# Lower bounds of a gated recurrence made as columns, and its first projection placed ahead of the compression of keys

## The chip, the cores and the metric

One core of a Trainium2 chip runs the whole program. The metric is the device time of one execution in microseconds (us). The core has five engines: PE (TensorE, the matrix products), DVE (VectorE), ACT (ScalarE), POOL (GpSimd) and SP (SyncE, which here only issues DMAs). Each takes its own instructions in order; semaphores make one wait for another.

## The reference

The program is three transformer-like blocks with a mixture of experts and a retrieval layer between them. The change lies in the mixer of the second block alone: 256 tokens of width 1024, an attention over compressed, selected and windowed keys, and beside it a gated recurrence.

```
lb_all = cumsum(softmax(hgrn_lb_logits, axis=0), axis=0)     # logits [2, 512]; row 0 is used
# compression of keys: blocks of positions + pos_emb, then gelu(flat @ w1) @ w2
# recurrence, 4 heads of 128, chunks of 32 tokens:
f = lb + (1 - lb) * sigmoid(hf);  k = 1 - f;  q = silu(hq)
b = cumsum(log f) in the chunk
o = tril(q e^b (k e^-b)^T) v + q e^b S
S = e^b_end * S + (k e^(b_end-b))^T v
o = rmsnorm(o) * norm_g * silu(hg)
y = g_a * (o_nsa @ w_branch[0]) + g_b * (o @ w_branch[1]);  out = y @ w_out
```

hq, hf, hi, hg and the two gates are columns of one projection of the normed input. With a softmax over two rows, lb is one row of 512 numbers, the same for every token.

## The kernel before

Activations lie with tokens on partitions (two halves of 128 tokens, index `a`). Every weight matrix comes by SP's queue in pieces of 1 MB into a ring of six buffers. `dense` takes one piece of 128x1024 at a time: ACT casts it to a rounded half `wh` (L151), DVE subtracts to get the rest `wl` (L152), and PE multiplies both with the split activations (L169: `pd<-wh,b`, `pd<-wl,b`, 128x512 each), 12 matmuls for a piece, 48 for a projection of 512 columns.

`block2` holds two generators. `attention()` begins with the key compression: transposes of keys (L1192, L1208), copies out of them into a padded tile (L1195 and L1213 on DVE), the addition of the position embedding (L1218, DVE), and 2 x 16 products with the first compression matrix (L1221; the DVE tile of L1218 is the weight side, so L1221 waits for it). Then come four head pairs of softmax and products. `recurrence()` first makes lb and 1 - lb in the scaled form `lb[0]`, `om` from two rows that DMAs spread over all partitions (L1333 to L1344), then four projections in the order f, q, v, g (`c` = 1, 0, 2, 3), and then for each half `a` the chunks: products with the state `S` (L1412, which waits for `S`), the update of `S` (L1417 on PE; L1419, L1420 on DVE), and at the end of the half a norm: Square on ACT (L1424), sum and scaling on DVE (L1426, L1427), a power on POOL (L1428), three products on DVE (L1430 to L1432), transposes on PE (L1435) and copies out of PSUM (L1438 ACT, L1439 DVE) into `OHT`. The four gate projections and the branch projections (L1462 on; `ONT`, the attention's output, and `OHT`, the recurrence's) follow.

Beside them runs `fill`: the next adaptive modulation, summed by ACT (L291), DVE (L292) and additions `acc + t` of 128x1024 (L294), of which six in eight are on POOL, and reduced by PE (L265, L270).

In what order the instructions of an engine stand is set by a scheduler that takes dependences and the order of the code; the code of the second block is written as `attention()` to its end, then `recurrence()` to its end, then gates. In the order of instructions a tile's name carries a number that differs between the two kernels.

Of the kernel before, what the change touches and what calls it, by code (L numbers as in the profile page):

```python
# [12 lines left out]
AF = mybir.ActivationFunctionType  # L13
ALU = mybir.AluOpType
AX = mybir.AxisListType
PSUM = bass.MemoryType.PSUM
P = 128
# [11 lines left out]
def bcast_rows(ap1d, n=P):  # L29

    return ap1d.unsqueeze(0).broadcast_to([n, ap1d.shape[-1]])
# [23 lines left out]
def step(gen, n):  # L55
    for _ in range(n):
        next(gen, None)


def body(tc, A, out, stages=("b1", "moe", "b2", "peer", "b3"), dbg=None):  # L60
# [31 lines left out]
    with Pool("cst") as cst, Pool("ring", bufs=RING) as ring, Pool("psum", nb={"ps": 4, "pd": 3, "pa": 1}, space=PSUM) as psp:  # L92
# [398 lines left out]
        if "b2" in stages:  # L491
            block2(K)
# [635 lines left out]
def block2(K):  # L1128
    nc, mm, pst, psd, A, x, ident, cst, Pool = K.nc, K.mm, K.pst, K.psd, K.A, K.x, K.ident, K.cst, K.Pool
    col, load, load8, mod = K.col, K.load, K.load8, K.mods[2]  # L1130
    nb = {"b8": 5, "b4": 5, "b2": 4, "h2": 7, "wh": 2, "wl": 2}
    with Pool("b2", nb=nb) as wp:
# [196 lines left out]
        lb = [wp("lb", [P, 512], bufs=2) for _ in range(2)]  # L1329

        def recurrence():
            for r in range(2):
                nc.sync.dma_start(lb[r], bcast_rows(A["hgrn_lb"][r]))  # L1333
            om = wp("h2", [P, 512])
            nc.vector.tensor_tensor(om, lb[0], lb[1], ALU.max)
            for r in range(2):
                nc.vector.tensor_tensor(lb[r], lb[r], om, ALU.subtract)
                nc.scalar.activation(lb[r], lb[r], AF.Exp)
            nc.vector.tensor_tensor(om, lb[0], lb[1], ALU.add)
            nc.vector.reciprocal(om, om)  # L1340
            nc.vector.tensor_tensor(lb[0], lb[0], om, ALU.mult)

            nc.vector.tensor_scalar(om, lb[0], -0.5, 0.5, ALU.mult, ALU.add)
            nc.vector.tensor_scalar(lb[0], lb[0], 0.5, 0.5, ALU.mult, ALU.add)  # L1344
            for c in (1, 0, 2, 3):
                w = load8(A["w_in_2"][2 + c])
                for a, ps in enumerate(K.dense(wp, [hT], w)):
# [7 lines left out]
                    else:  # L1355
                        d = (HQ if c == 0 else HG)[:, a, :]
                        t = wp("h2", [P, 512])
# [18 lines left out]
            for a in range(2):  # L1376
# [18 lines left out]
                for src, dst in ((qd, qdT), (ki, kiT)):  # L1395
                    pt = pst()
# [12 lines left out]
                for c in range(4):  # L1409
                    r = slice(32 * c, 32 * c + 32)  # L1410
# [22 lines left out]
                pt = pst()  # L1433
# [11 lines left out]
        def gates(h, j):  # L1445
# [3 lines left out]
            for a, ps in enumerate(K.dense(wp, [hT], w)):  # L1449
                nc.scalar.activation(G[j][:, a, h * 512 : (h + 1) * 512], ps, AF.Tanh, scale=0.5)  # L1450

        for _ in attention():
            pass
        for _ in recurrence():
            pass
        for h in range(2):
            for j in range(2):
# [4 lines left out]
        for h in range(2):  # L1462
            w = load8(A["w_branch"][h])
            for j, o in enumerate((ONT, OHT)):
                for a, ps in enumerate(K.dense(wp, [o], w, k0=4 * j, kt=4)):
                    m = M[:, a, h * 512 : (h + 1) * 512]
                    t = wp("b2", [P, 512]) if j else m
# [471 lines left out]
def _chunk(w, n=512):  # L1939

    k, m = w.shape
    return np.ascontiguousarray(w.reshape(k // P, P, m // n, n).transpose(2, 1, 0, 3))


def _cols(v):
    return np.ascontiguousarray(v.reshape(-1, P).T)
# [68 lines left out]
def layout(I):  # L2015
    f = lambda n: np.asarray(I[n])
    A = {}
    A["x"] = f("x")[0]
    A["ctx"] = f("ctx")[0]
    cols = []  # L2020
    for n in _COL_NAMES:
        v = f(n)
        if n in ("conv_w_3", "ffn_conv_w_3"):
            v = v[0].reshape(3, -1, P).transpose(2, 0, 1).reshape(P, -1)
        else:
            v = _cols(v.reshape(-1))
        cols.append(v)
    A["p_cols"] = np.ascontiguousarray(np.concatenate(cols, axis=1))
    A["w_ada"] = _chunk(f("w_ada")[0][:, 0:2048].reshape(D, 2, 4, 256).transpose(0, 2, 1, 3).reshape(D, 2048))
    A["w_ada_g"] = _chunk(f("w_ada")[0][:, 2048:], 2048)  # L2030
    A["b_ada"] = f("b_ada")[0]
    A["b_in"] = f("b_in")[0]
    A["w_in"] = _chunk(f("w_in")[0])
    A["attn_sink"] = f("attn_sink")[0]
    A["w_pool"] = np.ascontiguousarray(f("w_pool")[0].reshape(4, 2, P, T).transpose(2, 0, 1, 3))
    for n in ("w_attn_br", "w_pool_br", "w_out"):
        A[n] = _chunk(f(n)[0])
    A["w_router"] = np.ascontiguousarray(f("w_router")[0].reshape(8, P, 32).transpose(1, 0, 2))
    A["b_router"] = f("b_router")[0]
    A["b_gu"] = f("b_gu")[0]  # L2040
    A["b_down"] = f("b_down")[0]
    A["w_gu"] = np.ascontiguousarray(f("w_gu")[0].reshape(32, 8, P, 4, 512).transpose(0, 3, 2, 1, 4))
    A["w_down"] = np.ascontiguousarray(f("w_down")[0].reshape(32, 8, P, 2, 512).transpose(0, 3, 2, 1, 4))
    A["final_g"] = f("final_g")
    A["w_ada_2"] = _chunk(f("w_ada_2")[0], 2048)
    A["b_ada_2"] = f("b_ada_2")[0]
    w = f("w_in_2")[0]
    o = 512 + 768 + 24
    A["w_in_2"] = _chunk(np.concatenate([w[:, 0:1024], w[:, o : o + 4096]], axis=1))
    A["w_in_2b"] = np.ascontiguousarray(w[:, 1024:o].reshape(8, P, 280).transpose(1, 0, 2))  # L2050
    pe = np.stack([f("cmp_pos_k_2")[0], f("cmp_pos_v_2")[0]])
    A["cmp_pos"] = np.ascontiguousarray(pe.reshape(2, 16, P).transpose(2, 0, 1))
    A["w_c1"] = np.ascontiguousarray(np.stack([f("w_ck1_2")[0], f("w_cv1_2")[0]]).reshape(2, 16, P, P).transpose(0, 2, 1, 3))
    A["w_c2"] = np.ascontiguousarray(np.stack([f("w_ck2_2")[0], f("w_ck2_2")[0], f("w_cv2_2")[0]], axis=1))
    A["hgrn_lb"] = f("hgrn_lb_logits_2")
    A["hgrn_norm"] = f("hgrn_out_norm_2")[0]
    A["w_branch"] = _chunk(f("w_branch_2")[0].reshape(1024, D))
    A["w_out_2"] = _chunk(f("w_out_2")[0])
    A["w_peer_q"] = _chunk(f("w_peer_q_2")[0])
    A["peer_keys"] = np.ascontiguousarray(f("peer_sub_keys_2")[0].transpose(3, 1, 0, 2).reshape(P, 16, P))  # L2060
    u = f("peer_u_2")[0].reshape(P, 32, 4, 8, P)
    A["peer_u"] = np.ascontiguousarray(u.transpose(1, 4, 2, 3, 0).reshape(32, P, 4, D))
    A["peer_v"] = np.ascontiguousarray(f("peer_v_2")[0].reshape(P, 32, 4, D).transpose(1, 0, 2, 3))
    A["g_final_2"] = f("g_final_2")
    A["w_ada_3"] = _chunk(f("w_ada_3")[0], 2048)
    A["b_ada_3"] = f("b_ada_3")[0]
    A["w_in_3"] = _chunk(f("w_in_3")[0])
    A["w_out_3"] = _chunk(f("w_out_3")[0])
    w = f("w_up_3")[0].reshape(8, P, 2, 11, 2 * P)
    A["w_up_3"] = np.ascontiguousarray(w.transpose(3, 1, 0, 2, 4).reshape(11, P, 8, 512))  # L2070
    A["w_down_3"] = np.ascontiguousarray(f("w_down_3")[0].reshape(11, 2, P, D).transpose(0, 2, 1, 3))
    A["g_final_3"] = f("g_final_3")
    A.update(constants())
    return A
# [19 lines left out]
```

## Time and profile before

| | |
|---|---|
| median of three runs | 2760.5 us (2754.87 to 2763.53) |
| profiled execution | 2761.05 us, of which the span is 2759.3 us |
| busy over the span | PE 93%, DVE 56%, ACT 37%, POOL 8% |
| mean granted TensorE clock | 0.974 |
| DMA queue, share of 16 engines | 74.9% |

The second block's mixer lies between about 1280 and 1557 us of the span. A group of a timeline is several instructions of one kind that follow each other; the brackets at its end give how long the engine stood idle ahead of it and what it waited for. A granted clock of 1.00 is TensorE's level of 2.4 GHz, 0.50 its level of 1.2 GHz.

### The profile page before, as it was taken

The page shows a single profiled execution, that of the slowest core. Times are in us where ns is not written, and L with a number is a line of the kernel's source. Part 1 is how long each engine was busy: PE and PEld are TensorE (multiplying, and loading weights), DVE is VectorE, ACT ScalarE, POOL GpSimd, SP SyncE. Part 2 cuts the span into 40 slices and gives each one's busy share as a digit, 9 for nine tenths or more (in the row PEclk, how much of TensorE's full clock was granted, in tenths as well). Part 3 has the DMA queues.
Part 4 walks back from the last instruction along what each step waited for, and adds up shares of the span by engine and source line. Part 5 has one row for each costly group of instructions (what it writes and reads, how often), then busy time and mean ns, then how long its engine had stood idle before and what let it go on. Part 6 is the DMA issues. An engine that isn't in the chain of part 4 may idle for free. (4 is left out here: it accounts for less than half of the span.)

```text
span 2759.3 us, 36658 instructions
## 1 busy us (share of the span) xinstructions
PE 2572.4 (93%) x14235; PEld 1776.8 (64%) x14235; DVE 1532.0 (56%) x2573; ACT 1023.2 (37%) x1604; POOL 207.4 (8%) x125
## 2 busy tenths in 40 slices
PE   7999997999799969998999998999999999999998
PEld 4767741333133313333766897999888888888897
DVE  4997621122112202114787799697777675567777
ACT  3665300010001000002564433875555444455554
POOL 1221000000000000001112022100101000010000
PEclk9999999999999989999999999999999999999999
DMA  7669699999999999998565443678887775554452
GB/s 288 233 227 331 263 388 424 424 422 373 423 424 423 406 424 424 423 424 323 170 211 200 152 159 132 214 228 321 280 294 282 252 288 198 197 181 138 168 184 77
DMA packets 154016, 786.02 MB, mean 285 GB/s; under 512 B 14960, under 2 KB 49648, under 8 KB 70000
## 3 DMA queue, kind: packets, MB, share of 16 engines
q1 hardware_dynamic: 153840, 783.66, 74.9%
q8 instruction: 113, 1.85, 0.3%
q14 instruction: 63, 0.52, 0.0%
HBM read 765.78 MB, written 17.83 MB: 284 GB/s over the span
## 5 line engine op out<-in xcount | busy, mean ns | idle before, releaser
L152 DVE TENSOR_TENSOR wl<-w,wh 128x1024 fp32r<-128x1024 f32 x361 | 456.6, 1270 | 166.0 <-ACT wh L151 156.6
L151 ACT CAST wh<-w 128x1024 fp32r<-128x1024 f32 x379 | 393.8, 1044 | 344.1 <-PE pd L169 108.2
L169 PE MATMUL pd<-wh,b 128*128 128x512 f32 (+1 forms) x960 | 266.3, 395 | 2.2 <-POOL b L419 0.8
L936 PE MATMUL pd<-w,xd 128*64 128x512 f32 (+2 forms) x864 | 242.6, 601 | 4.6 <-DMA w<-in_w_gu 4.6
L169 PEld LDWEIGHTS pd<-wh,b 128*128 128x128 f32 x960 | 176.3, 189 | 48.0 <-issue 8.6
L1707 PE MATMUL pd<-wh,b 128*128 128x512 f32 x630 | 194.5, 390 | 0.2 <-ACT b L1691 0.2
L902 DVE TENSOR_SCALAR b<-pd 128x512 f32<-128x512 f32 x28 | 19.4, 692 | 254.5 <-PE pd L937 254.5
L169 PE MATMUL pd<-wl,b 128*128 128x512 f32 (+1 forms) x480 | 152.2, 396 | 5.8 <-DVE wl L152 5.7
L936 PEld LDWEIGHTS pd<-w,xd 128*64 128x64 f32 (+2 forms) x864 | 71.7, 132 | 113.9 <-issue 101.8
L936 PE MATMUL pd<-wB,xd 128*64 128x512 f32 (+2 forms) x392 | 137.0, 611 | 4.0 <-DMA wB<-in_w_gu 4.0
L955 DVE TENSOR_TENSOR b<-pd,g 128x512 f32<-128x512 f32 x28 | 19.3, 691 | 212.2 <-PE pd L937 212.2
L901 ACT ACTIVATE b<-b 128x512 f32<-128x512 f32 x28 | 17.7, 632 | 309.7 <-DVE b L900 309.7
L1707 PEld LDWEIGHTS pd<-wh,b 128*128 128x128 f32 x630 | 115.9, 188 | 22.9 <-ACT b L1691 0.4
L936 PE MATMUL pd<-w,at 128*64 128x512 f32 (+2 forms) x384 | 115.0, 646 | 14.1 <-DMA w<-in_w_down 13.4
L936 PE MATMUL pd<-wA,xd 128*64 128x512 f32 (+2 forms) x272 | 113.4, 647 | 4.9 <-DMA wA<-in_w_gu 4.9
L893 ACT ACTIVATE xd<-ps,mod,gs 128x128 f32<-128x128 f32 x56 | 25.3, 460 | 240.0 <-PE ps L889 160.2
L900 DVE TENSOR_SCALAR b<-pd 128x512 f32<-128x512 f32 x28 | 19.3, 690 | 165.1 <-PE pd L937 165.1
L169 PEld LDWEIGHTS pd<-wl,b 128*128 128x128 f32 x480 | 88.8, 189 | 28.3 <-DVE wl L152 8.3
L1707 PE MATMUL pd<-wl,b 128*128 128x512 f32 x315 | 105.5, 389 | 0.0
L1575 DVE TENSOR_TENSOR b<-iota,slt 128x512 f32<-128x512 f32 x128 | 87.1, 736 | 22.7 <-PE pd L1583 22.7
L1669 PE MATMUL ps<-b,wh 128*128 128x256 f32 x384 | 96.4, 292 | 2.8 <-ACT wh L151 2.8
L152 DVE TENSOR_TENSOR xT<-w,xT 128x1024 fp32r<-128x1024 f32 x53 | 66.3, 1251 | 55.9 <-ACT xT L151 55.9
(621 smaller groups left out, 5673.4 us busy)
## 6 DMA issues: line engine op xcount, KB each, us to landing
w<-in_w_gu SPq DMA_DIRECT2D x108, 1024.0 KB, 19.2
w<-in_peer_u SPq DMA_DIRECT2D x64, 1024.0 KB, 5.2
w<-in_peer_v SPq DMA_DIRECT2D x64, 1024.0 KB, 5.2
w<-in_w_down SPq DMA_DIRECT2D x59, 1024.0 KB, 19.6
w<-in_w_in SPq DMA_DIRECT2D x50, 1024.0 KB, 5.8
wB<-in_w_gu SPq DMA_DIRECT2D x49, 1024.0 KB, 19.6
w<-in_w_ada SPq DMA_DIRECT2D x48, 1024.0 KB, 6.0
wA<-in_w_gu SPq DMA_DIRECT2D x34, 1024.0 KB, 19.5
```

Of the source, the lines that this page charges most:

```text
L151: nc.scalar.copy(h, raw)
L152: (eng or nc.vector).tensor_tensor(l, raw, h.bitcast(F32), ALU.subtract)
L169: ins = mm(o, h[:, kk - k0 + k, a * P : (a + 1) * P], w[:, k * n : (k + 1) * n], start=(kk == k0 and m == 0 and k == 0), stop=(kk == k0 + ...
L893: nc.scalar.activation(d, s, AF.Identity, bias=sh[:, q : q + 1], scale=gs[:, q : q + 1])
L900: nc.vector.tensor_scalar(g, psg, 7.0, None, ALU.min)
L901: nc.scalar.activation(s, g, AF.Tanh, scale=0.851)
L902: nc.vector.tensor_scalar(l, psl, 7.0, -7.0, ALU.min, ALU.max)
L936: mm(ps[r], xt[:, k, r], ws[i][k // 4][:, k % 4, :], start=(k == 0), stop=False, skip_group_check=True)
L955: nc.vector.tensor_tensor(y, ps, g2[:, c * 512 : (c + 1) * 512], ALU.mult)
L1575: nc.vector.tensor_tensor(o, iota.unsqueeze(1).broadcast_to([P, 4, P]), SLT[:, v, t0 : t0 + 4].unsqueeze(2).broadcast_to([P, 4, P]), ALU.i ...
L1669: mm(o, wh[:, c], hh[:, k, :], start=(k == 0), stop=False)
L1707: ins = mm(acc[2 * a + c], p[:, i, a * P : (a + 1) * P], q[:, c * 512 : (c + 1) * 512], start=(first and i == 0 and n == 0), stop=(last an ...
```

## The change

The logits come as columns: one DMA brings a tile of 128 x 2 x 4, feature on partition. The softmax and the two scaled forms are worked out on 4 or 8 columns. Eight PE transposes of a column spread over 128 columns give the two rows on all partitions, and two ACT copies take them from PSUM to `lb[0]` and `om`. The generator of the recurrence is made before the attention's and taken one step, so that the lower bounds and the projection for f come ahead of the key compression in the code.

```
-            for r in range(2):
-                nc.sync.dma_start(lb[r], bcast_rows(A["hgrn_lb"][r]))
+            lc = wp("lc", [P, 2, 4])
+            nc.sync.dma_start(lc, A["hgrn_lb"])
+            mo = wp("lo", [P, 2, 4])
+            nc.vector.tensor_tensor(mo[:, 0, :], lc[:, 0, :], lc[:, 1, :], ALU.max)
+            nc.vector.tensor_tensor(lc, lc, mo[:, 0:1, :].broadcast_to([P, 2, 4]), ALU.subtract)
+            nc.scalar.activation(lc, lc, AF.Exp)
+            nc.vector.tensor_tensor(mo[:, 0, :], lc[:, 0, :], lc[:, 1, :], ALU.add)
+            nc.vector.reciprocal(mo[:, 0, :], mo[:, 0, :])
+            nc.vector.tensor_tensor(lc[:, 0, :], lc[:, 0, :], mo[:, 0, :], ALU.mult)
+            nc.vector.tensor_scalar(mo[:, 0, :], lc[:, 0, :], 0.5, 0.5, ALU.mult, ALU.add)
+            nc.vector.tensor_scalar(mo[:, 1, :], lc[:, 0, :], -0.5, 0.5, ALU.mult, ALU.add)
             om = wp("h2", [P, 512])
-            nc.vector.tensor_tensor(om, lb[0], lb[1], ALU.max)
...
-            nc.vector.tensor_scalar(om, lb[0], -0.5, 0.5, ALU.mult, ALU.add)
-            nc.vector.tensor_scalar(lb[0], lb[0], 0.5, 0.5, ALU.mult, ALU.add)
+            for r, t in enumerate((lb[0], om)):
+                pt = pst()
+                for k in range(4):
+                    nc.tensor.transpose(pt[:, k * P : (k + 1) * P], mo[:, r, k : k + 1].broadcast_to([P, P]), ident)
+                nc.scalar.copy(t, pt)
...
+        linear = recurrence()
+        step(linear, 1)
         for _ in attention():
             pass
-        for _ in recurrence():
+        for _ in linear:
             pass
...
-    A["hgrn_lb"] = f("hgrn_lb_logits_2")
+    A["hgrn_lb"] = np.ascontiguousarray(f("hgrn_lb_logits_2").reshape(2, 4, P).transpose(2, 0, 1))
```

In the changed file the lines of the recurrence have numbers 6 higher from its projections on (L1412 is L1418, L1435 is L1441), those behind `attention()`'s call 8 higher (L1468 is L1476). Outside the second block's mixer the order of instructions is the same on every engine.

On PE, at the key compression, this stands before. `b_1519` and `b_1520` are the two split halves of the input, `pd_7989` and `pd_7990` the projection that follows.

```order
L1192 MATMUL ps_7447<-ident_64,b_1532_7175 128x128 x4
L1192 MATMUL ps_7457<-ident_64,b_1532_7175 128x128 x4
L1208 MATMUL ps_7474<-ident_64,b_1533_7176 128x128 x4
L169 MATMUL pd_7989<-wh_7991,b_1519_7124 128x512 x2
L169 MATMUL pd_7989<-wh_7991,b_1520_7125 128x512 x2
L169 MATMUL pd_7990<-wh_7991,b_1519_7124 128x512 x2
L169 MATMUL pd_7990<-wh_7991,b_1520_7125 128x512 x2
L1221 MATMUL ps_7470<-w_7471,b_1601_7479 32x128 x16
```

The same place in the changed kernel, from the last transposes of keys to the first product of the compression; ahead of it stand the eight transposes of L1349 and the 48 matmuls for f.

```order
L1208 MATMUL ps_7574<-ident_64,b_1533_7176 128x128 x4
L169 MATMUL pd_8076<-wh_8078,b_1519_7124 128x512 x2
...
L169 MATMUL pd_8077<-wl_8095,b_1519_7124 128x512 x2
L169 MATMUL pd_8076<-wh_8110,b_1519_7124 128x512
L1221 MATMUL ps_7570<-w_7571,b_1618_7579 32x128 x16
```

Between L1208 and L1221 there were 8 matmuls, and there are 25 now.

On POOL, between the key compression and the end of the recurrence, the additions of `fill` and the recurrence's memsets (L1400) and powers (L1428) stood like this before.

```order
L294 TENSOR_TENSOR b_1529_7170<-b_1529_7170,w_8595 128x1024
L294 TENSOR_TENSOR b_1824_8617<-b_1824_8617,w_8693 128x1024
L294 TENSOR_TENSOR b_1824_8617<-b_1824_8617,w_8698 128x1024
L1400 MEMSET h_1766_8325 128x512
L294 TENSOR_TENSOR b_1844_8720<-b_1844_8720,w_8795 128x1024
L294 TENSOR_TENSOR b_1844_8720<-b_1844_8720,w_8800 128x1024
L1428 TENSOR_TENSOR ss_8400<-ss_8400,mhalf_70 128x4
L294 TENSOR_TENSOR b_1863_8822<-b_1863_8822,w_8897 128x1024
L1400 MEMSET h_1791_8436 128x512
L294 TENSOR_TENSOR b_1863_8822<-b_1863_8822,w_8902 128x1024
L1428 TENSOR_TENSOR ss_8503<-ss_8503,mhalf_70 128x4
```

In the changed kernel they stand like this.

```order
L294 TENSOR_TENSOR b_1828_8628<-b_1828_8628,w_8709 128x1024
L294 TENSOR_TENSOR b_1848_8731<-b_1848_8731,w_8806 128x1024
L294 TENSOR_TENSOR b_1848_8731<-b_1848_8731,w_8811 128x1024
L294 TENSOR_TENSOR b_1867_8833<-b_1867_8833,w_8908 128x1024
L294 TENSOR_TENSOR b_1867_8833<-b_1867_8833,w_8913 128x1024
L1406 MEMSET h_1770_8336 128x512
L1434 TENSOR_TENSOR ss_8411<-ss_8411,mhalf_70 128x4
L1406 MEMSET h_1795_8447 128x512
L1434 TENSOR_TENSOR ss_8514<-ss_8514,mhalf_70 128x4
```

Four of the eight additions have moved from the recurrence to ahead of it, into the head pairs of the attention.

On PE, at the end of the recurrence's second half, this stood before; `oT_7434` and `oT_7435` are `ONT`, `b_1519` belongs to a gate projection.

```order
L1412 MATMUL ps_8456<-S_8494,h_1789_8434 32x128 x4
L169 MATMUL pd_8830<-wl_8880,b_1519_7124 128x512
L306 MATMUL pd_8913<-ident_64,mod_9_83 128x128 x4
L306 MATMUL pd_8919<-ident_64,mod_9_83 128x128 x4
L169 MATMUL pd_8930<-wh_8932,oT_7434 128x512 x2
...
L169 MATMUL pd_8930<-wh_8948,oT_7435 128x512
L1435 MATMUL ps_8510<-ident_64,h_1802_8501 128x128 x4
```

In the changed kernel `oT_7436` and `oT_7437` are `OHT`; `pd_8987` and `pd_8988` are its branch projection for the two halves.

```order
L1418 MATMUL ps_8467<-S_8481,h_1793_8445 32x128 x4
L1423 MATMUL ps_8500<-hp_7440,h_1792_8438 128x128 x4
L169 MATMUL pd_8987<-wl_9006,oT_7436 128x512
L1418 MATMUL ps_8467<-S_8493,h_1793_8445 32x128 x4
L1418 MATMUL ps_8467<-S_8505,h_1793_8445 32x128 x4
L1441 MATMUL ps_8521<-ident_64,h_1806_8512 128x128 x4
L373 MATMUL ps_9109<-ident_64,b_1886_8936 128x128
L373 MATMUL ps_9116<-ident_64,b_1886_8936 128x128
L169 MATMUL pd_8988<-wh_8989,oT_7436 128x512 x2
```

The gate projections and the whole branch projection of `ONT` stand ahead of this place now, and between the last product with `S` and the transposes of the norm's result nothing is left.

On DVE, the same place in the changed kernel: L1425 and L1426 make `S`, L1432 to L1438 are the norm, L1476 and L1478 take a branch projection out of PSUM.

```order
L1425 TENSOR_TENSOR S_8493<-S_8481,dec_8434 128x512
L1426 TENSOR_TENSOR S_8493<-S_8493,ps_8488 128x512
L1476 SCALAR_TENSOR_TENSOR b_1903_9021<-b_1829_8631,pd_8987 128x512
L1425 TENSOR_TENSOR S_8505<-S_8493,dec_8434 128x512
L1478 TENSOR_TENSOR b_1886_8936<-b_1886_8936,b_1903_9021 128x512
L1426 TENSOR_TENSOR S_8505<-S_8505,ps_8500 128x512
L1432 TENSOR_REDUCE ss_8514<-h_1806_8512 128x4
```

L1476 has come between the steps of `S`, and it reads `pd_8987`, whose last matmul is the single L169 of the PE rows.

## Rows read from the trace of the kernel before

**Rows 1.** Windows: busy us of engines (instructions), PEclk, DMA share, GB/s.

```profile
1280.00:1557.00 277.00, 251.38 (x1298) 190.94 (x1296) 215.86 (x401) 139.71 (x240) 44.01 (x31) 0.97 0.56 194
1334.00:1337.00 3.00, 3.00 (x17) 2.48 (x15) 2.87 (x8) 0.36 (x1) 0.00 (x0) 0.50 0.00 0
1469.00:1471.00 2.00, 2.00 (x8) 1.15 (x7) 0.40 (x1) 0.00 (x0) 0.00 (x0) 0.50 1.03 418
```

**Rows 2.** Waits of PE, 1280 to 1600 us: total us, times, longest.

```profile
PE ps L1221 <- DVE b L1218: 4.0, 1, 4.0
```

**Rows 3.** Timeline of PE at the key compression: start, us, instructions, [idle before].

```profile
1325.91 1.04 PE L1192 MATMUL ps<-ident,b 128*128 128x128 f32 x8
...
1333.21 5.35 PE L1221 MATMUL ps<-w,b 128*32 128x128 f32 x32 [3.97 <-DVE b L1218]
...
1343.49 3.65 PE L1221 MATMUL ps<-w,b 128*32 128x128 f32 x32 [0.49 <-issue]
```

**Rows 4.** Timeline of PE in the attention; from the first start to the second, 24 matmuls.

```profile
1355.17 1.08 PE L169 MATMUL pd<-wh,b 128*128 128x512 f32 x4
...
1360.63 1.07 PE L169 MATMUL pd<-wh,b 128*128 128x512 f32 x4
```

**Rows 5.** Timeline of DVE ahead of the first L1221.

```profile
1331.82 0.43 DVE L1195 COPY b<-ps 64x256 f32<-64x256 f32 x1
1332.28 0.88 DVE L1218 TENSOR_TENSOR b<-b,pe 128x120 f32<-128x120 f32 x3
```

**Rows 6.** DMAs of 1280 to 1400 us: KB each, us to landing.

```profile
hm<-in_c_hmask SPq DMA_DIRECT2D x1, 4.0 KB, 5.4
```

**Rows 7.** Timeline of PE in the recurrence.

```profile
1465.34 1.06 PE L1412 MATMUL ps<-S,h 128*32 128x128 f32 x8 [2.27 <-DVE S L1420]
...
1467.88 1.65 PE L169 MATMUL pd<-wh,b 128*128 128x512 f32 x3
...
1473.89 0.62 PE L169 MATMUL pd<-wl,b 128*128 128x512 f32 x2
...
1478.42 1.05 PE L265 MATMUL pa<-b,ones 128*32 128x512 f32 x4
...
1480.76 0.46 PE L270 MATMUL pa<-ident,b 64*128 64x64 f32 x4
...
1498.18 1.06 PE L1412 MATMUL ps<-S,h 128*32 128x128 f32 x8 [1.09 <-DVE S L1420]
...
1504.62 1.06 PE L1412 MATMUL ps<-S,h 128*32 128x128 f32 x8
...
1511.58 0.66 PE L1435 MATMUL ps<-ident,h 128*128 128x128 f32 x4 [1.03 <-DVE h L1432]
```

**Rows 8.** Timeline of the other engines in the norm of the second half.

```profile
1505.72 0.60 ACT L1424 ACTIVATE h<-ps 128x512 f32<-128x512 f32 x1
...
1506.22 1.23 DVE L152 TENSOR_TENSOR wl<-w,wh 128x1024 fp32r<-128x1024 f32 x1 [3.38 <-PE pd L169]
1507.37 0.68 DVE L1426 TENSOR_REDUCE ss<-h 128x4 f32<-128x512 f32 x1
...
1510.83 0.69 DVE L1432 TENSOR_TENSOR h<-h,hp 128x512 f32<-128x512 f32 x1
```

**Rows 9.** Timeline of all engines around a pair of L294 in the attention.

```profile
1429.03 5.82 POOL L294 TENSOR_TENSOR b<-b,w 128x1024 f32<-128x1024 f32 x2 [36.08 <-DVE b L292]
...
1431.38 4.55 DVE L152 TENSOR_TENSOR wl<-w,wh 128x1024 fp32r<-128x1024 f32 x2
...
1435.99 0.73 PE L169 MATMUL pd<-wl,b 128*128 128x512 f32 x2 [1.23 <-DVE wl L152]
```

**Rows 10.** Timeline of POOL and DVE, 1379 to 1464 us.

```profile
1381.26 2.40 POOL L294 TENSOR_TENSOR b<-b,w 128x1024 f32<-128x1024 f32 x1 [48.97 <-DVE mx L1296]
...
1455.79 6.62 POOL L294 TENSOR_TENSOR b<-b,w 128x1024 f32<-128x1024 f32 x2 [20.47 <-DVE b L292]
1458.35 5.14 DVE L152 TENSOR_TENSOR wl<-w,wh 128x1024 fp32r<-128x1024 f32 x2
```

More of the change, by code (lines that the diff above doesn't have):

```diff
@@ L1331, in recurrence @@
         def recurrence():
-            for r in range(2):
-                nc.sync.dma_start(lb[r], bcast_rows(A["hgrn_lb"][r]))
-            om = wp("h2", [P, 512])
-            nc.vector.tensor_tensor(om, lb[0], lb[1], ALU.max)
[L1336 to L1341, printed above, removed]
-            nc.vector.tensor_scalar(om, lb[0], -0.5, 0.5, ALU.mult, ALU.add)
-            nc.vector.tensor_scalar(lb[0], lb[0], 0.5, 0.5, ALU.mult, ALU.add)
+            lc = wp("lc", [P, 2, 4])
[9 more added lines that the diff above has]
+            nc.vector.tensor_scalar(mo[:, 1, :], lc[:, 0, :], -0.5, 0.5, ALU.mult, ALU.add)
+            om = wp("h2", [P, 512])
+            for r, t in enumerate((lb[0], om)):
[3 more added lines that the diff above has]
+                nc.scalar.copy(t, pt)
             for c in (1, 0, 2, 3):
```

## The prediction

> **What bounds the kernel now.** The page's summary comes first: PE is busy for 93% of the span, so only what PE waits for, what it is given to do and the clock it gets can move the end. The windows come next. In the second block's mixer PE is busy for 251.38 of 277 us and DVE for 215.86 [rows 1]; PE is still the bound, but DVE is close enough behind that a chain of DVE steps can hold it up. The layer that follows is a long PE stretch, so what the mixer's PE loses or gains arrives at the end of the program unshortened.
>
> The list of PE's waits is read third. The largest one in the mixer is 4.0 us at the key compression, L1221 waiting for DVE's L1218 [rows 2]. The timelines then show what stands around the waits. At 1333.21 the first L1221 group begins after 3.97 us of idling, and it takes 5.35 us where the second group of the same 32 takes 3.65 [rows 3]: the granted clock in 1334 to 1337 is 0.50, the 1.2 GHz level [rows 1]. In the recurrence L1412 waits 2.27 and 1.09 us for S and L1435 1.03 us for the norm [rows 7], and after the first of these the clock is 0.50 again [rows 1]. So an idle PE pays twice here, first by the wait and then by slow matmuls.
>
> **The change, part by part.**
>
> *A, the key compression.* Before, 8 matmuls stood between the last transposes of keys and the first L1221. They were not enough to cover the chain on DVE, which had to finish work on whole rows for the lower bounds (L1339 to L1344) at the same time. Now 25 matmuls stand there, with the 48 of the projection for f ahead of them. What goes: the wait of 3.97, the slow clock 5.35 - 3.65 = 1.70, and the 0.49 ahead of the second group [rows 3], in all 6.16 us. What comes: eight transposes, priced by eight of the same shape at 1.04 [rows 3], and what is left of the wait. A 512-column matmul takes (1360.63 - 1355.17) / 24 = 0.2275 us [rows 4], so 25 give 5.69 us of cover. On DVE there stand in that time, by the order, two products and sums of the new projection at 0.69 (priced by L1432 [rows 8]), seven copies or scalings at 0.43 and four L1218 at 0.88 / 3 [rows 5], and a split of which I count half, 1.23 / 2 [rows 8]: 1.38 + 3.01 + 1.17 + 0.6 = 6.2 us. The remaining wait is 0.5 to 0.6; bounds are none, and the old 3.97 with its 1.70. A = -6.16 + 1.04 + 0.6 = -4.5.
>
> The rest of the lower bounds is hidden: DVE and ACT now handle 4 or 8 columns and two copies in place of nine passes over 512 columns, and PE did not wait for those passes where they began. The columns' DMA is new, and the first step on DVE that reads it stands ahead of other work of the block. A transfer of like size lands in 5.4 us [rows 6], and it is issued about 10 us ahead of its reader; if that cover were gone, DVE would start some us late at a place where PE has its own long wait for the norm.
>
> *B, first half of the recurrence.* Before, two POOL additions (6.62 us) and two DVE splits (5.14 us) lay in the chain of S [rows 10], and the L1412 at 1465.34 waited 2.27 [rows 7]. From 1467.88 to 1473.89 PE did 9 matmuls and one L1412 group in 6.01 us; at full clock they are 9 x 0.2275 + 1.0 = 3.04, so the slow clock cost 3.0. Now all POOL additions are over before the recurrence begins, and in DVE's order the steps of S follow one another. Removed: 2.27 + 3.0 = 5.3. Added: the norm of the first half is now wanted early. Its chain without the split in it is 4.85 us (worked out under C); in DVE's new order L1476 (0.69), one split (1.23) and L273 (0.16, a guess from its width of 8) have come between its steps, and perhaps part of another split, which makes 7.3. Ahead of L1441 PE has 13 matmuls (2.96), L265 (1.05) and L270 (0.46) [rows 7]: 4.5. The wait is 2.9 (bounds 0, where DVE runs early, to 4.5), and the clock behind it costs 0 to 3.0; I take 1.5. B = -5.3 + 2.9 + 1.5 = -0.9.
>
> *C, end of the recurrence.* The waits of 1.09 and 1.03 [rows 7] go with the order that had them: -2.1. In the new order nothing covers this place: the gates and the branch projection of the attention's output, which lay beside the norm before, have been used up earlier. First, the last S: from the last matmul into `pd_8987`, DVE does L1476, L1425, L1478 and L1426, four times 0.69 and 0.3 of gaps, while PE has one L1418 of 1.06: a wait of 2.0. Then the norm: before, it took from the end of L1412 at 1504.62 + 1.06 = 1505.68 to L1435 at 1511.58 [rows 7], 5.90 us, in which a split held L1426 from 1505.72 + 0.60 to 1507.37, 1.05 us [rows 8]. That leaves 4.85, uncovered. Then two copies into `OHT` before the second half of the branch projection can start; the order has PE's L373 transposes beside a part of them, so 0.75 of some 1.3. In all 7.6 to 7.7; bounds 5 and 9. The clock behind so long an idle time falls to 0.50 as it did at 1334 and 1469 and costs 1.7 (as in A) to 3.0 (as in B); I take 2.3. C = -2.1 + 7.7 + 2.3 = +7.9.
>
> *D, the attention.* Four POOL additions move here. Before, one pair lay here, at 1429.03, and two DVE splits beside it took 4.55 us [rows 9], where one alone takes 1.23 [rows 8]; PE waited 1.23 for the second [rows 9]. Two more pairs at something over half that bite are +1.5. Bounds: 0, where no split falls beside them, and 9.6, where DVE stands still for each addition at 2.40 [rows 10]. The trace bears on how the two engines share: the splits lost 4.55 - 2 x 1.23 = 2.1 us against additions of 5.82, so they waited for a part of the pair only. The Trainium skill (SBUF — State Buffer, Who interferes with whom) says that a DVE instruction with two SBUF inputs contends with a GpSimd instruction that reads SBUF, and that the shared ports are held for a whole instruction; by that rule each added addition may block a split of DVE for all of its length, which is the upper bound here, and the row of the stretched splits agrees that they collide.
>
> *Sum.* A -4.5, B -0.9, C +7.9, D +1.5: +4.0 us on the profiled execution's 2761.05, so 2765.05. That execution lies 0.55 above the median of the runs shown (2760.5), so the forecast is 2764.5 us. The gain in the compression is real but is spent at the end of the recurrence.
>
> **The rivals.**
>
> *R1, faster: the norms find their cover.* If DVE and ACT run far enough ahead of PE in the recurrence, neither half's norm is waited for and the clock stays up. Then C loses 10.0 and B 4.4, and the time is 2764.5 - 14.4 = 2750.1. For it speaks that the recurrence's DVE steps are now free of POOL's additions; against it, that the order has no PE work at all between the last product with S and the norm's transposes, and a chain over three engines cannot take nothing.
>
> *R2, slower: POOL's additions block DVE in the attention.* The place is the splits ahead of L169 between 1340 and 1455; the price is the bound of D, 9.6 instead of 1.5, so 2772.6. It decides if the added additions find DVE in splits each time and PE waits more than about 2 us for each. For it speaks the pair at 1429.03; against it, that the other addition in this stretch, at 1381.26 [rows 10], led to no wait of PE for a split.
>
> *R3, slower: the compression gains nothing.* If DVE's new products (they wait for the new projection) hold up the copies of keys, the first L1221 waits as before. Then A is +0.55, from the transposes less the 0.49, and the time is 2769.6. Against it speaks the cover of 5.69 us, three times what was there.
>
> **How the numbers follow.** What a measurement of this kernel can tell from no change is about 0.3%, 8.3 us, so "same" is 2752.2 to 2768.8. The forecast's own range follows from the bounds of B and C, 2757 to 2771. Chances: forecast 0.55 (0.47 same, 0.08 slower), R1 0.18 (0.13 faster, 0.05 same), R2 0.15 (all but 0.02 slower), R3 0.12 (0.07 slower, 0.05 same). In sum 0.13 faster, 0.59 same, 0.28 slower. The range of 8 in 10 takes in the forecast's own, most of R2 and R3 and the upper part of R1: 2752 to 2775.
>
> **What the profile would show.** A is right if the first L1221 group begins after less than 1.5 us of idling and takes about 3.65; it is wrong if the list of PE's waits still has L1221 near 4. C is right if PE's longest wait in the mixer is now L1441 for L1438, near 5 us, with L1418 waiting about 2 for S right ahead of it and a granted clock of 0.50 behind. B is right if L1441 has a second wait near 3 and L1418 in the first half none above 0.5. D is right if L169 waits for L152 in the attention for 1 to 3 us more than the 1.23. The forecast falls if the waits of L1441 come to under 3 in all (then R1), or if those for L152 come to over 6 (then R2).

## The result and the profile after

The changed kernel takes 2783.34 us (median of 4 runs, 2779.57 to 2787.48), the kernel before 2758.85 us: a ratio of 1.0073, 95% interval 1.0059 to 1.0088. The medians differ by 24.5 us, the ratio stands for some 20; the forecast was 2764.5 with a range to 2775. The profiled execution took 2781.55 us, its span is 2779.7 us, 20.4 more than before, at the same mean granted clock of 0.974.

First the list of PE's waits in the second block of the kernel after (total us, times, longest). It answers to [rows 2].

```profile
...
PE ps L1310 <- DVE b L1308: 7.6, 3, 3.7
PE ps L1441 <- DVE h L1438: 7.0, 2, 5.0
...
PE pd L169 <- DVE wl L152: 3.7, 4, 1.3
PE ps L1269 <- DVE cs L1267: 3.4, 1, 3.4
PE ps L1418 <- DVE S L1426: 2.0, 3, 1.6
```

L1221 for L1218 has left the list, as forecast, and L1441 and L1418 have come, as forecast. L1310 and L1269, the transposes behind the softmax of the attention, were in no term of the sum.

To see what each part is worth, the mixer is cut into four stretches that hold the same stages in both kernels: up to the first scores of the compressed keys (L1253), the attention, the recurrence with its norms, and the rest up to the next layer's first matmul (L194). Columns as in [rows 1]; first before, then after.

```profile
1289.25:1352.00 62.75, 54.59 (x293) 44.87 (x293) 49.02 (x83) 27.53 (x47) 15.36 (x16) 0.94 0.57 200
1352.00:1451.50 99.50, 95.36 (x483) 68.01 (x481) 83.02 (x216) 63.42 (x130) 11.01 (x5) 1.00 0.57 192
1451.50:1513.00 61.50, 56.89 (x328) 43.66 (x327) 47.72 (x57) 27.21 (x38) 16.49 (x7) 0.94 0.60 220
1513.00:1565.35 52.35, 47.29 (x215) 37.36 (x213) 36.64 (x49) 21.63 (x26) 1.38 (x2) 0.94 0.42 142
```

```profile
1290.43:1363.30 72.87, 70.60 (x362) 58.33 (x363) 53.09 (x95) 37.44 (x61) 17.37 (x16) 0.93 0.60 208
1363.30:1490.00 126.70, 112.76 (x522) 78.05 (x520) 104.82 (x224) 70.48 (x136) 24.12 (x9) 0.93 0.64 223
1490.00:1545.00 55.00, 44.98 (x271) 34.68 (x270) 28.37 (x45) 12.67 (x21) 2.51 (x3) 0.88 0.11 42
1545.00:1587.55 42.55, 37.23 (x169) 30.00 (x167) 29.88 (x40) 17.85 (x22) 1.38 (x2) 0.96 0.44 150
```

The lengths can't be compared, since projections have moved between stretches, but idle time and slow clock can. Idle is the length less PE's busy time. The loss by the clock is PE's busy time times (1 - granted clock), summed over windows of 1 us.

| stretch | idle before, after | clock loss before, after | change |
|---|---|---|---|
| to the compression | 8.2, 2.3 | 3.2, 4.7 | -4.4 |
| attention | 4.1, 13.9 | 0.0, 8.0 | +17.8 |
| recurrence | 4.6, 10.0 | 3.4, 4.2 | +6.2 |
| rest | 5.1, 5.3 | 1.9, 1.6 | -0.1 |

With 1.03 us for the eight transposes that makes 20.5 of the 297.12 - 276.10 = 21.0 us by which the four stretches together have grown. Half of it is waiting and half is the clock. (Of the 4.7 in the first row all lies at the block's start, where PE's order is that of before: there the clock stayed at 0.50 until 1301 us in this execution and until 1293 in the one before. These 3.2 us are not the change's: over the traces of this document the loss at the block's start is 1.5 to 2.3 us in eight and 4.6 to 4.7 in six, 1.5 in e2 with the step ahead and 4.7 in e4 without it.)

The attention is where the forecast failed. PE's waits add up to nearly all of its idle time there: for splits (L169) 1.5 us before and 2.9 after, for the softmax chains (L1269 and L1310) 2.4 and 11.0. The timeline of all engines around the longest of its waits, after:

```profile
1412.42 4.80 POOL L294 TENSOR_TENSOR b<-b,w 128x1024 f32<-128x1024 f32 x2 [28.87 <-DVE b L292]
1412.54 2.30 DVE L1301 TENSOR_SCALAR sm<-sm 128x4 f32<-128x4 f32 x1 [0.25 <-ACT b L1300]
...
1414.87 0.18 DVE L1302 RECIPROCAL sm<-sm 128x4 f32<-128x4 f32 x1
1415.08 2.23 DVE L1304 TENSOR_TENSOR sm<-sm,gl 128x2 f32<-128x2 f32 x2
1417.28 0.87 DVE L1308 TENSOR_SCALAR b<-b,sm 128x128 f32<-128x128 f32 x4
...
1417.71 0.88 PE L1310 MATMUL ps<-ident,b 128*128 128x128 f32 x3 [3.75 <-DVE b L1308]
```

L1301 works on 128x4 numbers and takes 2.30 us. It ends at 1414.84, and the first of POOL's two additions, of 2.38 us, ends at 1414.80; L1304 ends at 1417.31, the second addition (1414.88, 2.34 us) at 1417.22. DVE's step stands still until POOL's addition ends. Meanwhile PE's last L169 ends at 1413.96, and it has nothing else before L1310. The other waits have the same neighbours: L1261 takes 2.44 us beside an addition, ahead of the 3.40 us of L1269, and two more steps of L1301 take 2.37 ahead of the later waits of L1310 (0.90 and 2.91 us). In the lines of DVE in the attention of the changed kernel (times, busy us, mean ns) these steps stand out:

```profile
L1301 DVE TENSOR_SCALAR sm<-sm 128x4 f32<-128x4 f32 x8 | 7.9, 985 | 2.7 <-ACT b L1300 2.7
...
L1261 DVE TENSOR_TENSOR cs<-cs,cm 128x128 f32<-128x128 f32 x2 | 2.7, 1366 | 0.4 <-ACT cs L1260 0.4
```

The same lines of the kernel before, where four additions lie in the attention (all eight do after the change) and none met one of these steps:

```profile
L1301 DVE TENSOR_SCALAR sm<-sm 128x4 f32<-128x4 f32 x8 | 1.3, 166 | 4.5 <-ACT b L1300 4.4
...
L1261 DVE TENSOR_TENSOR cs<-cs,cm 128x128 f32<-128x128 f32 x2 | 0.6, 292 | 0.5 <-ACT cs L1260 0.4
```

One addition of the kernel before did hold another small softmax step, L1296, to its end:

```profile
1390.55 2.41 POOL L294 TENSOR_TENSOR b<-b,w 128x1024 f32<-128x1024 f32 x1 [6.89 <-DVE w L292]
...
1391.09 1.90 DVE L1296 TENSOR_SCALAR mx<-mx 128x4 f32<-128x4 f32 x1
```

Alone L1296 takes 0.16 to 0.17 us; a second one took 1.09 at 1430.37. Neither cost PE a wait, since matmuls of L169 stood beside both. So a held step costs time where PE has run out of other work, as at 1413.96.

Behind each of the waits after the change PE runs slow, two of the four places:

```profile
1386.00:1388.00 2.00, 2.00 (x7) 1.53 (x6) 1.94 (x11) 0.00 (x0) 0.00 (x0) 0.50 1.04 414
1418.00:1420.00 2.00, 2.00 (x8) 1.29 (x6) 0.89 (x3) 1.42 (x2) 0.00 (x0) 0.50 1.00 393
```

The compression and the end of the recurrence came out as worked out. The timeline of PE there, after, answers to [rows 3] and [rows 7]:

```profile
1346.88 3.68 PE L1221 MATMUL ps<-w,b 128*32 128x128 f32 x32
...
1512.96 1.11 PE L1441 MATMUL ps<-ident,h 128*128 128x128 f32 x4 [2.08 <-DVE h L1438]
...
1531.03 1.06 PE L1418 MATMUL ps<-S,h 128*32 128x128 f32 x8 [1.59 <-DVE S L1426]
1537.05 1.08 PE L1441 MATMUL ps<-ident,h 128*128 128x128 f32 x4 [4.97 <-DVE h L1438]
```

The first L1221 waits for nothing and runs at full clock. The waits of 2.08, 1.59 and 4.97 us were forecast as 2.9, 2.0 and 4.85 us.

### The profile page after: what moved, and what is told of

The parts are those of the page before. It is cut to its first block, busy times and chain, and to the rows that moved or that the text cites. A ratio compares the mean times of both kernels' runs of the same rounds, so it can differ in the third digit from the quotient of the medians.

```text
span 2779.7 us, 36677 instructions
## 1 busy us (share of the span) xinstructions
PE 2576.6 (93%) x14243; PEld 1778.1 (64%) x14243; DVE 1532.3 (55%) x2572; ACT 1019.8 (37%) x1604; POOL 208.6 (8%) x125
## 5 line engine op out<-in xcount | busy, mean ns | idle before, releaser
L152 DVE TENSOR_TENSOR wl<-w,wh 128x1024 fp32r<-128x1024 f32 x361 | 453.9, 1263 | 176.1 <-ACT wh L151 165.8
L169 PE MATMUL pd<-wh,b 128*128 128x512 f32 (+1 forms) x960 | 267.7, 396 | 1.5 <-DVE f L1872 0.6
L169 PEld LDWEIGHTS pd<-wh,b 128*128 128x128 f32 x960 | 177.7, 190 | 48.0 <-issue 7.5
L169 PE MATMUL pd<-wl,b 128*128 128x512 f32 (+1 forms) x480 | 151.4, 395 | 6.0 <-DVE wl L152 5.9
L169 PEld LDWEIGHTS pd<-wl,b 128*128 128x128 f32 x480 | 89.9, 190 | 29.0 <-DVE wl L152 8.6
L152 DVE TENSOR_TENSOR xT<-w,xT 128x1024 fp32r<-128x1024 f32 x53 | 64.9, 1224 | 54.6 <-ACT xT L151 54.5
```

Of the source, the lines that this page charges most:

```text
L152: (eng or nc.vector).tensor_tensor(l, raw, h.bitcast(F32), ALU.subtract)
L169: ins = mm(o, h[:, kk - k0 + k, a * P : (a + 1) * P], w[:, k * n : (k + 1) * n], start=(kk == k0 and m == 0 and k == 0), stop=(kk == k0 + ...
```

## The experiments

**Theory:** POOL's additions, pushed into the attention by the step ahead, stop DVE's small steps there, and each stop costs PE a wait and a stretch at 0.50. **Rivals:** the softmax chains lack cover because the projection for f has left the attention; or the columns and their transposes cost the time.

### The two parts of the change apart

The first kernel has the columns, with the step ahead taken back; the second has the step ahead over the lower bounds of before.

```
e1:  for _ in attention(): pass          # columns as in the change
     for _ in recurrence(): pass
e2:  linear = recurrence(); step(linear, 1)   # lower bounds on rows, as before
```

> The lower bounds as columns and transposes, but the recurrence's generator taken after the attention as before. If the loss of 24 us sits in the step ahead (its effect on the attention), this kernel should stay near the kernel before, 2756 to 2762 us. Rival, from the order of instructions: the eight transposes now stand on PE behind the last head pair, so the projection for f cannot be taken out of PSUM and no projection of the recurrence can lie inside the attention; then the softmax chains have nothing beside them and PE idles some 50 us: 2800 to 2850 us, with L1310 as the longest total wait.

> The step ahead alone, lower bounds on rows as before. Theory (the eight POOL additions stand inside the attention, and each pair holds DVE's softmax steps): the additions have the same places on POOL as in the changed kernel, so 2778 to 2785 us, with waits of L1269 and L1310 of 8 to 12 us in all. Rival (the columns and their transposes cost the time): 2755 to 2762 us.

The columns alone took 2820.11 us (1.021, 1.0194 to 1.0226), as the rival of their expectation had it. PE's waits in that kernel:

```profile
PE ps L1310 <- DVE b L1308: 26.8, 7, 5.6
```

The eight transposes stand on PE at 1446.6 us there, behind the last L1310 (1445.6), and no projection that needs the bounds can be finished before them: beside the attention PE has some 67 matmuls of L169, where it had 257 before. So the transposes need the step ahead, or another early place. The step ahead alone took 2780.74 us (1.0072, 1.0056 to 1.0087), the changed kernel's time. Its waits:

```profile
PE ps L1310 <- DVE b L1308: 7.6, 3, 3.8
PE ps L1435 <- DVE h L1432: 7.1, 2, 5.0
...
PE ps L1269 <- DVE cs L1267: 3.4, 1, 3.4
```

These three are those of the changed kernel to a tenth. L1221 no longer waits here either (0.3 us), so the step ahead alone covers the compression too. The columns are not the cause; the moved step is.

### POOL's additions taken away

```
-  (nc.vector if k == 6 else nc.gpsimd).tensor_tensor(acc, acc, t, ALU.add)
+  (nc.vector if k == 6 or tag == "b8" else nc.gpsimd).tensor_tensor(acc, acc, t, ALU.add)
```

In the changed kernel (e3) and in the kernel before (e4), for the second block alone.

> The changed kernel with the six POOL additions in eight of the second block's modulation sums done by DVE. Theory (POOL's additions stretch the small DVE steps of the softmax chains from 0.2 to 2.3 us): L1301, L1304 and L1261 fall to 0.2 to 0.5 us, the waits of L1269 and L1310 from 11.0 to 2 to 4 us and the slow clock behind them goes; 8 x 1.21 us more on DVE give back 2 to 4 us: 2768 to 2774 us. Rival (the chains lack cover since the projection for f has left the attention): the waits stay at 9 to 12 us and the time at 2783 us or up to 10 us above.

> The kernel before with the same additions on DVE. Theory: the pair at 1429 us and the pair at 1456 us no longer stretch DVE's steps, so the wait of L1412 at 1465 us with its slow clock (5.3 us) and most of 1.5 us go, DVE's 9.7 us more give back 1 to 4: 2753 to 2757 us. Rival (DVE is too full for them): 2762 to 2768 us.

The changed kernel with it: 2765.64 us (1.0018, 1.0008 to 1.0028), some 15 us less than 1.0073 stands for, and 2.4 us below the theory's range. The waits of L1269 and L1310 fell from 11.0 to 1.1 us, and the lines of DVE in its attention read:

```profile
L1301 DVE TENSOR_SCALAR sm<-sm 128x4 f32<-128x4 f32 x8 | 1.3, 168 | 1.9 <-ACT b L1300 1.8
...
L1261 DVE TENSOR_TENSOR cs<-cs,cm 128x128 f32<-128x128 f32 x2 | 0.6, 289 | 0.4 <-ACT cs L1260 0.4
```

The projection for f is still ahead, and the chains have cover enough: the theory holds, and the rival of the missing cover falls as a cause by itself. Cut at the same places, e3's attention has 3.5 us of idling and no slow clock (13.9 and 8.0 in the changed kernel). The eight more passes on DVE, which I had priced at 2 to 4 us, left PE's waits for splits in the mixer at 3.2 us in all. The kernel before with it: 2756.72 us (0.9982, 0.997 to 0.9994), in the theory's range; L1412's waits fell from 3.4 to 0.4 us, L1435's rose from 1.0 to 2.5. Without POOL's additions the change costs about 9 us; what stands out in the list of e3's waits is the recurrence (L1441 8.1, L1418 2.0 us). Up to 7 us behind its last transposes the recurrence has 15.4 us of idling and slow clock in e3 and 4.9 in e4.

### The additions on POOL, but later

```
             for j in range(2):
                 gates(h, j)
-                step(fill, 4)
+        step(fill, 16)
```

> The changed kernel with the sixteen steps of the modulation sum written behind the four gates instead of four behind each, POOL still doing six of eight additions. In the order POOL's additions now stand beside the recurrence, two of the eight at its beginning, none inside the head pairs. Theory (POOL's additions beside the softmax chains make the waits): L1269 and L1310 fall from 11.0 us of waiting to under 3, but DVE's steps of S and of the norms are stretched instead, L1418 and L1441 wait 3 to 6 us more than 9.0: 2768 to 2776 us. Rival (the projection's matmuls are missing as cover in the attention): L1269 and L1310 still wait 9 to 12 us, 2783 us or more.

2767.49 us (1.0023, 1.0012 to 1.0034), 0.5 us below the theory's range; its waits are as the theory had them. PE's waits:

```profile
PE ps L1441 <- DVE h L1438: 10.6, 2, 8.7
...
PE ps L1418 <- DVE S L1426: 1.8, 3, 0.9
PE ps L1310 <- DVE b L1308: 1.7, 3, 0.9
```

L1269 is gone from the list, and the norm pays instead, 10.6 for 7.0. Two additions still lie inside the head pairs, other than expected: at 1427.04 and 1437.63 each holds an L1296, for 1.80 and 2.48 us, and PE, with matmuls of L169 beside them, waits for neither. The same additions cost by what they stand beside.

### The sum without POOL and with less of ACT

```
-  activation(t, w0 * s); t = w1 * s' + t; acc = acc + t
+  acc = w0 * s + acc;    acc = w1 * s' + acc        # both on DVE
```

> The changed kernel with the modulation sum as two multiply-adds on DVE for each piece, nothing of it on POOL and only the first piece of a sum on ACT. DVE has as many 128x1024 passes as in the kernel with all additions on DVE, ACT 1.15 us less for each piece. If POOL alone made the waits: 2762 to 2768 us, as with all additions on DVE. Rival (ACT's queue in the softmax chains matters too): 2755 to 2761 us.

2769.15 us (1.0022, 1.0013 to 1.0031), 1.2 us above the first range, 8 above the rival's, and no better than e3. One wait of 5.39 us stands ahead of the last head pair's transposes, with no POOL instruction beside it:

```profile
1473.35 1.94 PE L1313 MATMUL ps<-ident,b 128*128 128x128 f32 x8 [5.39 <-DVE b L1311]
```

In e3 PE has eight matmuls of L306 and seven of L169 between the products ahead of this place and L1310; here it has none from 1467.96 us on. So a softmax chain that has nothing beside it makes PE wait without POOL too; the additions are the cause of the waits in the changed kernel, not the only possible one. Why the scheduler placed the matmuls otherwise is open.

### Cover for the end of the recurrence

The branch projection is written output by output, and its second part for the attention's output is held until the third product with `S` of the second half. In the changed kernel with additions on DVE (e11) and in the kernel before with them (e13):

```
+  for j, o in enumerate((ONT, OHT)):
+      for h in range(2):
+          w = [load(A["w_branch"][h][:, 4 * j : 4 * j + 4, :])] * 2
+          with after_all(K, (K.held.ins,) if (h, j) == (1, 0) else ()):
+              pa = K.dense(wp, [o], w, k0=4 * j, kt=4)
```

> The changed kernel with all additions on DVE, the branch projection written output by output (both column halves of the attention's output first), and the second of these held behind the third product with S of the second half. Theory (what is left of the loss is the uncovered end of the recurrence, L1418 1.6 and L1441 5.0 us with slow clock behind them, together 8 to 11 us): these two waits go, but the 24 matmuls are taken from the first half's end, where L1441 now waits up to 5: 2756 to 2763 us. Rival (the cover is only moved, every matmul held here is missed there): 2763 to 2768 us, as without the hold.

> The kernel before with all additions on DVE, the same order of the branch projections and the same hold. Theory: the one wait left at the end of the recurrence (L1435 2.5 us) goes and nothing else changes: 2752 to 2756 us against 2756.7 without the hold. Rival (the held matmuls are missed earlier): 2757 to 2762 us.

The changed kernel: 2760.96 us (0.999, 0.9979 to 1.0001), in the theory's range. L1441's (here L1443's) 8.1 us of waiting became 3.9; the first half's norm kept 3.1 of it, as the order let one expect. The kernel before: 2751.72 us (0.9961, 0.9949 to 0.9974), 0.3 us below its theory's range and 0.2% under e4, with no wait in the recurrence above 0.43 us; no kernel here has a lower ratio. Between these two kernels only the change of this document differs, and it costs 0.3%: 9.2 us, where it cost 8.9 between e3 and e4. The hold helps both kernels about alike, so it takes away the wait at the end (5.0 us became 0.8) but not what the change costs. Idling and slow clock of the recurrence still differ by 7.4 us (8.3 and 0.9).

### The lower bounds ahead, the projection left in place

```
             nc.scalar.copy(t, pt)
+            yield
```

The first step now ends behind the lower bounds, and the projections come after `attention()`. On the kernel before (e15) and on e13 (e14).

> The kernel before with only the lower bounds changed and taken ahead: columns, eight transposes and two copies stand ahead of the key compression, the projection for f stays behind it; POOL's additions stand as in the kernel before. Theory (the columns are worth what the compression waits, the loss came with the moved projection): L1221 waits under 1.5 us in place of 4.0 and its first group takes 3.65 in place of 5.35, L1269 and L1310 wait as before (2.4 us in all), less 1.04 us for the transposes: 3 to 5 us below the kernel before. Rival (the 8 matmuls of before are not the cover, the copies of keys are late by themselves): L1221 still waits 3 to 4 us and the time is that of before or 1 us above.

> The same lower bounds in the kernel that has all additions on DVE and the held branch projection (0.9961 of before). If the two gains add, since they lie at different places of the mixer: another 3 to 5 us, a ratio of 0.994 to 0.995. Rival (a place that is covered now loses its cover to the earlier one): 0.996 to 0.998.

2760.46 us (0.9997, 0.9987 to 1.0007) and 2752.78 us (0.9964, 0.995 to 0.9977): nothing gained, against both theories (e14 lies in its rival's range), though 16 matmuls now stand ahead of L1221 in place of 8. The timeline of all engines in e15 shows why:

```profile
1329.63 2.75 POOL L516 TENSOR_TENSOR b<-b,rt 128x256 f32<-128x256 f32 x2 [0.87 <-ACT h L1349]
...
1332.33 0.94 POOL L1188 MEMSET b<- 128x1024 f32 x1
...
1333.30 0.37 ACT L1194 COPY b<-ps 64x256 f32<-64x256 f32 x1 [3.10 <-POOL b L1188]
...
1336.41 1.89 PE L1221 MATMUL ps<-w,b 128*32 128x128 f32 x11 [2.95 <-ACT b L1194]
```

The wait has a second cause behind the first: POOL clears the padded keys (L1188) only after the rope's products (L516), and ACT's copies, among them those for L1218, queue behind the one that waits for that memset. In the changed kernel POOL clears the keys from 1333.54 to 1335.39, ahead of the transposes of keys (1339.47), with matmuls of the projection for f in between, and L1221 does not wait.

Two last kernels, built on e14, put that memset on DVE (e16), and held the first branch projection of `ONT` too, behind the first half's last product with `S` (e17).

```
-  nc.gpsimd.memset(KB[v], 0.0)
+  nc.vector.memset(KB[v], 0.0)
```

> The kernel with early bounds, additions on DVE and the held branch projection, and the memsets of the padded keys (L1188) on DVE instead of POOL. Theory (the first L1221 still waits 2.9 us because POOL's memset stands behind the rope products of L516 on POOL, and ACT's copy waits for the memset): the wait goes to under 1 us. In the order five matmuls more have come ahead of L1221 and are missing beside the start of the recurrence's second half, which costs 1 to 5 us: 2747 to 2755 us. Rival (the copies of keys are late for another reason): L1221 still waits 2 to 3 us.

> The same with the first branch projection of the attention's output held too, behind the last product with S of the first half, so that it covers that half's norm. Theory (covers only have to be where the chains are): L1443's first wait falls from 3 to under 1 us and the last head pair of the attention, which loses nothing in the order, waits as before: 2745 to 2751 us. Rival (the held matmuls are missed before): 2752 to 2758 us, with L1310 or L169 waiting 3 us or more in the last head pair.

2755.23 us (0.9981, 0.9971 to 0.9992) and 2751.48 us (0.9973, 0.9961 to 0.9984). L1221 still waits 1.9 us in both, by the profile for nothing that it shows, so neither side of e16's expectation is met. L1269 waits 2.2 in place of 0.5. e17's time falls between its two ranges. L1443's waits are 0.2 and 0.8 in both kernels, and as far as their records go both traces show the same order on PE from the attention to the second norm, so the second hold moved nothing there and e17 does not test it; e13 with neither edit is as fast or faster.

## Why the prediction was wrong

*A, the compression* (-4.5): right in kind. The idle time of the first stretch fell by 5.9 us and the slow clock of the first L1221 (1.7) went; less 1.03 for the transposes that is -6.6, since the wait of 0.6 that A kept did not come and smaller waits went too. (The 3.2 us that the clock at the block's start took back belong to no part of the change.) But the wait's cause was only half read: the DVE chain of the lower bounds and POOL's queue each stood behind L1221, and e15 shows that removing the first leaves 2.95 us.

*B and C, the recurrence* (-0.9 + 7.9 = +7.0): right, +6.2 measured. The waits in them made +6.2 (idle time: +5.4), the clock +0.8 (measured: +0.8). Reading the order against the durations of [rows 8] gave each wait within 0.9 us. That what is left without POOL's additions lies here is shown by e3 against e4, 15.4 and 4.9 us; e11 takes the end's wait away, but its hold is worth about as much in the kernel before.

*D, the attention* (+1.5): this step failed. It measured +17.8. The step read "Two more pairs at something over half that bite are +1.5. Bounds: 0 [...] and 9.6, where DVE stands still for each addition". What it priced came as priced: PE's waits for splits rose by 1.4 us. Three things were wrong in it. First, it looked for the additions' victims among the splits of 1.23 us alone, and put PE's waits behind the softmax chains (L1269, L1310: +8.6) at nothing without a reason; there DVE steps of 0.15 to 0.3 us, once two in a row, each held until an addition ended, lie on a chain for which PE waits directly. Second, it counted three of the four additions in the attention before. The one that it left out, at 1390.55, held a small softmax step (L1296, 1.90 us), as the pair's first did (1.09); so the trace of before showed the kind of meeting, though at places where PE had other work. That none of the four met L1301 or L1261 there was the luck of that order. Third, its upper bound was too low: it counted DVE's standstill, not the slow clock behind each wait, which is 8.0 of the 17.8. e3 shows that the additions are the cause, e6 that it is their place.

R2 named the cause, with 0.15 and 2772.6 us, and its direction was right; its price, its place (the splits) and its sign in the profile (waits for L152 over 6 us; they came to 3.7) were not. D's own sign, 1 to 3 us more for splits, was met and told nothing of the rest. The sentence beside D that cites the Trainium skill (SBUF — State Buffer, Who interferes with whom), that the shared ports are held for a whole instruction, is borne out by the ends at 1414.84 and 1414.80, and for a step with one input in SBUF too (L1301); the same section says that `tensor_scalar` can enter a mode that uses the shared pair. Whether L1301 ran in that mode no run here shows.

## What to carry to other kernels

When a change moves work between stages, look at what the scheduler moves with it on POOL and DVE. Here a large elementwise step on POOL cost PE nothing beside a held step of the softmax as long as PE had other matmuls (L1296 before and in e6), and a wait where it had none (L1301, L1304, L1261). As an upper estimate, price such a meeting at one whole POOL instruction for each DVE step on the chain, take off the matmuls that PE has beside it, and add the matmuls at half clock that follow PE's wait. Independent matmuls are a stock: taken forward to cover 4 us of waiting, they are missing at the next chain, so hold some back where the last chain ends.

## What the runs showed of the hardware

A DVE step of 128x4 with one input took 2.30 us beside a POOL addition and 0.16 without, ending within 0.1 us of the addition; a reciprocal of 128x4 that began 0.01 us ahead of the second addition took its usual 0.18 us. PE waits of 2.08 to 4.97 us were followed by stretches at 0.50 in which it was fully busy, and so was one of 0.90 us at 1456 us of the changed kernel, which had waits of 1.28 and 0.78 us in the 5 us ahead of it. At the block's start, after the same 8.1 us of idling, the clock came back at 1293 us in one execution and at 1301 in another; the cause is open.
